# Softmax over rows of 512: issuing each tile's store in the middle of the next tile's exponentials

## The chip, the cores and the metric

The kernel runs on one core of a Trainium2 chip. The metric is the device time in microseconds (us). A profile covers one execution; its span is about 1.7 us shorter than the timed figure of the same run (160.3 against 162.04 us in the profiled run of the kernel before), because it counts from the first to the last profiled event.

## The reference

```python
x = randn(16, 1024, 512)                     # float32
s = x / 0.5
e = exp(s - max(s, axis=-1))
out = e / sum(e, axis=-1)                    # float32
```

16,384 rows of 512 numbers are read and written once: 33.55 MB in, 33.55 MB out.

## The kernel before

The rows are eight chunks (c) of 128 partitions x 16 rows, 4 MB each. Six buffers hold them, so chunks 6 and 7 reuse the buffers of chunks 0 and 1, and their loads wait until stores 0 and 1 have landed. VectorE takes each row's maximum (`shift`), ScalarE the exponentials with their sums, one row at a time, VectorE the reciprocals and the scaling of 7/8 of the rows, ScalarE the scaling of the rest. Loads are issued from the sync engine's queue (q1 in the profile), stores from ScalarE's (q10), as an instruction in ScalarE's own program. So the place of the store in that program decides when it can go out at the earliest.

```python
LOADS = [[(0, 4), (4, G)]] + [WHOLE] * 7
BLOCKS = [[(0, 4), (4, 8), (8, G)]] + [WHOLE] * 6 + [[(0, 8), (8, G)]]
STORES = [WHOLE] * 8
...
def rows(i):
    c, lo, hi = blocks[i]
    cut = hi - lo - (2 if c == 1 else 0)
    return range(cut), range(cut, hi - lo)

exponentials(0, rows(0)[0])
for i in range(n):
    if i + 1 < n:
        exponentials(i + 1, rows(i + 1)[0])   # ScalarE, rows ahead of the cut
    scale_vector(i)                           # VectorE: reciprocal, multiply
    scale_scalar(i)                           # ScalarE: the last 1/8 of the rows
    if i + 2 < n:
        shift(i + 2)                          # VectorE: maximum, bias
    store(i)                                  # issued from ScalarE
    if i + 1 < n:
        exponentials(i + 1, rows(i + 1)[1])   # ScalarE, rows behind the cut
```

## Time and profile before

| | kernel before |
|---|---|
| time, median of its first 3 runs | 162.27 us (162.05 to 162.5) |
| span of the profile | 160.3 us |
| VectorE busy, ScalarE busy | 134.6 us, 102.2 us |
| both DMA queues, share of the span | 49.4% + 48.5% |
| moved | 67.13 MB, 419 GB/s over the span |

A row of 40 digits gives the busy share of each fortieth of the span in tenths (9 is 90% or more). The chain that ended last is the work followed back from the last instruction, at each step to what released it; the line gives its time by engine. In an instruction line the columns are start, duration, engine (DVE is VectorE, ACT ScalarE, SPq and ACTq the queues of issued DMAs), source line, operation, output <- input, shapes, count; a bracket at the end tells how long the engine had been idle and what ended the wait. A queue's line gives packets, MB and the share of the 16 DMA engines' time; a packet counts where it starts, so the share of a short window can be a tenth or two off, and over 100%. A DMA issue's line ends with its size and the microseconds from issue to landing, so landing time is the issue's start plus that figure.

### The profile page before, as it was taken

How to read it: one execution, taken by the hardware profiler on the slowest of the kernel's cores; microseconds unless marked ns; L12 is line 12 of the kernel's file. 1: busy time of each engine (PE TensorE's matmuls, PEld its weight loads, DVE VectorE, ACT ScalarE, POOL GpSimd, SP SyncE). 2: the span in 40 equal slices, each digit the busy share in tenths (PEclk: the TensorE clock that was granted, in tenths of full speed). 3: DMA queues.
4: the chain of work that ended last, by engine and by line, in shares of the span. 5: the costliest groups of instructions: out<-in, count | busy, mean ns of one | idle time of the engine just before them, and what ended most of it. 6: DMA issues, size and time to landing. Idle time of an engine off the chain costs nothing.

```text
span 160.3 us, 402 instructions
## 1 busy us (share of the span) xinstructions
DVE 134.6 (84%) x45; ACT 102.2 (64%) x273; POOL 0.2 (0%) x4
## 2 busy tenths in 40 slices
DVE  0607999999999999999999999999999999957000
ACT  3071549069989972998199909991899891690000
POOL 0000000000000000000000000000000000000000
DMA  5999999999999999999999999999999999999993
GB/s 180 474 409 491 409 401 483 425 393 452 458 393 401 393 425 474 409 393 499 417 393 474 442 393 468 442 393 442 474 393 417 491 401 401 491 417 401 466 442 139
DMA packets 2450, 67.13 MB, mean 419 GB/s; under 512 B 272, under 2 KB 272, under 8 KB 272
## 3 DMA queue, kind: packets, MB, share of 16 engines
q1 hardware_dynamic: 1296, 33.56, 49.4%
q10 hardware_dynamic: 1152, 33.55, 48.5%
q14 instruction: 2, 0.02, 0.0%
HBM read 33.55 MB, written 33.55 MB: 419 GB/s over the span
## 4 chain that ended last, share of the span: by engine, by line
DVE 80%; DMA 7%; ACT 4%; issue 0%; SPq 0%
DVE negmax L74 42%; DVE xt L103 36%; DMA xt<-in_x_dram 7%; ACT xt L86 4%; DVE bias L78 1%; DVE recip L101 1%; SPq L66 0%
## 5 line engine op out<-in xcount | busy, mean ns | idle before, releaser
L86 ACT ACTIVATE xt<-xt,bias 128x512 f32<-128x512 f32 x128 | 90.4, 708 | 41.5 <-DVE bias L78 40.6
L74 DVE TENSOR_REDUCE negmax<-xt 128x16 f32<-128x8192 f32 (+2 forms) x11 | 69.9, 6353 | 9.5 <-DMA xt<-in_x_dram 9.5
L103 DVE TENSOR_TENSOR xt<-xt,recip 128x7168 f32<-128x7168 f32 (+2 forms) x11 | 62.0, 5637 | 0.4
L86 ACT ACTIVATION_READ_ACCUMULATOR xt<-xt,bias 128x1 f32 x128 | 23.9, 187 | 0.0
L112 ACT ACTIVATE xt<-xt,recip 128x512 f32<-128x512 f32 x15 | 9.9, 707 | 0.0
L101 DVE RECIPROCAL recip<-sums 128x16 f32<-128x16 f32 (+2 forms) x11 | 2.4, 218 | 1.8 <-ACT xt L86 1.8
L78 DVE TENSOR_SCALAR bias<-negmax 128x16 f32<-128x16 f32 (+2 forms) x11 | 1.9, 173 | 0.4
L52 ACT ACT_TABLE_LOAD x1 | 1.3, 1283 | 0.7 <-PEq L157 0.7
L51 DVE MEMSET warm<- 128x1 f32 x1 | 0.1, 59 | 0.8 <-PEq L157 0.8
L52 ACT ACTIVATE warm<-warm 128x1 f32<-128x1 f32 x1 | 0.2, 202 | 0.0
L157 POOL MEMSET const-bfloat16-1.0<- 128x1 bf16 x1 | 0.1, 101 | 0.0
L157 POOL MEMSET const-uint8-127<- 128x1 uint8 x1 | 0.1, 101 | 0.0
L157 POOL MEMSET const-float32-0.0<- 128x1 f32 x1 | 0.1, 98 | 0.2 <-issue 0.2
L157 POOL MEMSET const-float32-1.0<- 128x1 f32 x1 | 0.1, 98 | 0.0
## 6 DMA issues: line engine op xcount, KB each, us to landing
out_dram<-xt ACTq DMA_DIRECT2D x8, 4096.0 KB, 22.8
xt<-in_x_dram SPq DMA_DIRECT2D x7, 4096.0 KB, 30.1
xt<-in_x_dram SPq DMA_DIRECT2D x1, 3072.0 KB, 11.7
xt<-in_x_dram SPq DMA_DIRECT2D x1, 1024.0 KB, 4.8
```

Source lines behind the costliest of these rows:

```text
L51: nc.vector.memset(warm, 0.0)
L52: nc.scalar.activation(out=warm, in_=warm, func=EXP)
L74: nc.vector.tensor_reduce(negmax[:, 0:b], chunks[c][:, lo:hi, :], axis=AX, op=MAX, negate=True)
L78: nc.vector.tensor_scalar_mul(biases[i][:, 0:b], negmax[:, 0:b], 2.0)
L86: nc.scalar.activation(out=row, in_=row, func=EXP, bias=biases[i][:, g : g + 1], scale=2.0, accum_out=sums[i][:, g : g + 1],)
L101: nc.vector.reciprocal(recips[i][:, 0:b], sums[i][:, 0:b])
L103: nc.vector.tensor_mul(rows, rows, recips[i][:, 0:k].unsqueeze(2).broadcast_to((P, k, D)))
L112: nc.scalar.activation(out=row, in_=row, func=COPY, scale=recips[i][:, g : g + 1])
L157: nc = _bacc.Bacc("TRN2", target_bir_lowering=False, num_devices=1)
```

## The change

The intent: the store of a chunk (the title's tile) becomes ready once VectorE has scaled its share. The kernel before issues it behind all 16 exponentials of the next chunk (14 for chunk 1). The change cuts the list after 9 rows (5 for chunk 1), about when VectorE is through.

```diff
     def rows(i):
         c, lo, hi = blocks[i]
-        cut = hi - lo - (2 if c == 1 else 0)
-        return range(cut), range(cut, hi - lo)
+        cut = 5 if c == 1 else 9
+        return range(min(cut, hi - lo)), range(min(cut, hi - lo), hi - lo)
```

## The prediction

> **What bounds the kernel now.** I read the page's busy line, then the chain of work that ended last, then the transfers.
>
> ```profile
> DVE 134.6 (84%) x45; ACT 102.2 (64%) x273; POOL 0.2 (0%) x4
> ...
> DVE  0607999999999999999999999999999999957000
> ...
> DMA  5999999999999999999999999999999999999993
> ...
> DVE 80%; DMA 7%; ACT 4%; issue 0%; SPq 0%
> ```
>
> Two resources are full at once. The chain that ended last runs through VectorE (DVE): after 12.8 us it has only one wait of note, 1.8 us for the last exponentials, until the last multiply ends at 147.42 us. The DMA row is nines from the second slice of 4 us to the last but one. The second row is the harder bound: 67.13 MB at 419 GB/s is 160.2 us, the whole span. The chain alone suggests that an earlier store could not matter; the DMA row says that it can't create bandwidth, but can change who gets it.
>
> Next I read the sharing while loads (q1) and stores (q10) are both pending, 50 to 110 us:
>
> ```profile
> DMA packets 894, 26.12 MB, mean 435 GB/s; under 512 B 96, under 2 KB 96, under 8 KB 96
> ...
> q1 hardware_dynamic: 447, 13.07, 50.5%
> q10 hardware_dynamic: 446, 13.04, 50.3%
> ```
>
> The split is equal. So each load of 4 MB takes about 20 us here, where alone it takes about 10. Landing is issue plus time to landing, asked of the transfers in small windows. For the last load, of chunk 7, a window around 87.5 us gives
>
> ```profile
> xt<-in_x_dram SPq DMA_DIRECT2D x1, 4096.0 KB, 28.4
> ```
>
> which is 87.53 + 28.4 = 115.9 us. VectorE first needs that chunk here:
>
> ```profile
> 112.96 7.63 DVE L103 TENSOR_TENSOR xt<-xt,recip 128x7168 f32<-128x7168 f32 x1
> 120.50 4.41 DVE L74 TENSOR_REDUCE negmax<-xt 128x8 f32<-128x4096 f32 x1
> 124.95 0.17 DVE L78 TENSOR_SCALAR bias<-negmax 128x8 f32<-128x8 f32 x1
> 125.03 0.25 DVE L101 RECIPROCAL recip<-sums 128x16 f32<-128x16 f32 x1
> 125.31 7.63 DVE L103 TENSOR_TENSOR xt<-xt,recip 128x7168 f32<-128x7168 f32 x1
> ```
>
> The multiply in front of the reduction is what holds it until 120.50, so the load has 120.50 - 115.9 = 4.6 us to spare. By the same sums load 6 (issued 68.16, 27.7 us) lands at 95.9 and is needed at 103.88: 8.0 us to spare. Loads 1 to 3 land before any store, and loads 4 and 5 at about 57 and 77, needed at 70.65 and 87.26.
>
> At the other end the last two stores are issued at 133.03 and 147.50 and take 16.7 and 11.9 us, so they land at 149.7 and 159.4. The gap, 9.7 us, is a 4 MB transfer at full rate (4.19 MB at 434 GB/s). So at 147.50 the slowest DMA engine still had some 2 us of the store before to finish: the last store found no idle DMA, and VectorE and DMA end almost level.
>
> **What the Trainium skill says.** "DMA: Bandwidth & Descriptors", section "Queues, rings and completion order", says that each DMA engine serves the queues that have work in turn, packet by packet; the 50.5% against 50.3% agrees. Its section "Anatomy of one DMA" says that a DMA's semaphore wait is taken on the issuing sequencer before dispatch. So a store placed among ScalarE's (ACT's) exponentials holds up those behind it until VectorE's multiply is done. The trace of before has such a wait once: the last store's, 3.9 us behind the multiply that starts at 143.53; there nothing follows it. "ScalarE: Activation LUTs", section "What ACT_TABLE_LOAD costs", gives 280 ns + 0.833 ns per element for an ACTIVATE with a pointer bias, 706 ns at 512; the trace has 708.
>
> **The change, part by part.** No instruction is added or removed. Only the place at which ScalarE's list of exponentials of the next block is cut changes: 9 of 16 rows before the two copies and the store, 7 after. For chunk 1 it is 5 of 16 in place of 14. Blocks of 4 or 8 rows stay whole, so the stores of chunks 6 and 7 keep their place in the program.
>
> - Store 0: a row advances ScalarE by 0.705 us (708 + 187 ns, less the overlap; 16 rows from 46.33 to 57.62). Nine rows fewer lie before it, 9 x 0.705 = 6.35 us. It is issued at 44.11 - 6.35 = 37.76, and the multiply that it waits for ends at 37.49: no wait.
> - Stores 1 to 5: seven rows fewer, 4.9 us. Store 1: nine rows from 46.33 end at 52.7, two copies end at 54.0, the multiply ends at 54.10, so issue at about 54.2 in place of 58.97. The remaining seven rows then end at about 59.6, still before the next bias at 62.74. ScalarE waited 4.0 us for that bias before, so its lost time there is hidden.
> - Chunk 6 is the exception. Its successor is a half block, whose reduction takes 4.41 us instead of 8.68. Nine rows from 112.81 end at 119.2, copies at 120.5, the store waits for the multiply (end 120.59), issue 120.67 to 121.05, seven rows more (4.94 us) end at about 126.05. VectorE's reciprocal stands at 125.03 and needs these sums. So it waits some **1.0 us**, where before the sums were there at 124.1.
> - Loads: from the time at which store 0 begins, they get half the rate. It begins 6.35 us earlier and the store queue stays full (stores are issued every 16.6 us and take 19.4 at half rate). In 6.35 us loads lose half of what they moved, and later win it back at half rate: the end of the load stream moves by 6.35 us, one for one. Load 7: 115.9 + 6.35 = 122.25, against 120.50: a wait of **1.75 us**. Load 6: 102.25 against 103.88, still in time by 1.6. The buffers are no limit: store 0 lands at about 62 and store 1 at 81, so loads 6 and 7 can be issued before their forerunners are through.
>
> The two delays don't add. A reduction that starts at 122.25 ends at 126.66, and the reciprocal that follows finds its sums ready at 126.05. So VectorE's chain is late by the larger one, 1.75 us, and the last store is issued at about 149.25 instead of 147.50. The bytes moved up to then are the same in any order, so store 6 still lands near 149.7 to 150. The last store then arrives at a nearly idle DMA. If it lost nothing it would land at 150 + 9.7 = 159.7; if it starts cold, it takes what the first chunk took from nothing, 12.8 - 0.73 = 12.07 us, and lands at 161.3. So the end moves by 0.3 to 1.9 us. I take 1.5, as the issue at 149.25 leaves under 1 us of cover for a start-up of about 2.4 (12.07 - 9.7): 162.27 + 1.5 = **163.8 us**.
>
> **The rivals.**
> 1. *Earlier stores fill idle DMA time and the kernel gets faster.* For it speaks the idle share of the two queues, 100 - 49.4 - 48.5 = 2.1%, 3.4 us. Against it: most of that is the start, before 1.1 us plus latency, and the tail after 158 us, where only completions are left. Between 13 and 147 us hardly a window has a DMA share under 0.95. It would give at most some 0.5 us, so 161.8.
> 2. *The load of chunk 7 stays in time, and only ScalarE's late sums count.* If stores take hold less strongly, so that the load moves under 5 us, then VectorE loses 1.0 us and the end moves by 0 to 1.0: about 162.8. The load's margin, 4.6 against a shift of 6.35, makes this the less likely case.
> 3. *Loads 6 and 7 both come late, or the longer mixed phase costs bandwidth.* The mixed phase grows by about 13 us (6.35 at each end). Its 435 GB/s is that of stores alone (4.19 MB in 9.7 us, 434), so little speaks for that. With 1.6 us of margin gone on load 6 and 2 us more on load 7 it would be 165 to 166.
> 4. *ScalarE becomes the bound because it stalls at each store.* It is busy 64%, and has about 4 us to spare in each full block against a stall of 0.2: excluded except at chunk 6.
>
> **Range and chances.** Rival 1 gives 161.8, rival 2 162.8, the main path 162.6 to 164.2, rival 3 165 or more; the runs of before spread 0.45 us. Range 162.1 to 165.0. Faster by 2% means under 159.0, less than the transfers alone need: 0.01. Slower by 2% means over 165.5, which takes rival 3: 0.05. Within 2%: 0.94.
>
> **What the changed profile would show.** Store 0 issued near 37.8, stores 1 to 5 each about 4.9 us earlier than now. Load 7 landing near 122.2. In VectorE's waits a new one on the input transfer at chunk 7's first reduction, about 1.75 us; if that is absent, a wait of the reciprocal on ScalarE of about 1.0 us near 126. The last store issued near 149.2 with landing after 12 us. DMA still nines, 417 GB/s or so. The prediction is wrong if the mixed phase has another rate than the pure ones, if the equal split does not begin with the issue of store 0, or if the last store's start-up is hidden after all.

## The result, and the profile after

| | before | after |
|---|---|---|
| median time | 162.33 us (6 runs) | 163.36 us (6 runs, 163.13 to 163.59) |
| ratio | | 1.0063, 95% interval 1.005 to 1.0076 |
| span of the profile | 160.3 us | 161.4 us |
| store 0 issued | 44.11 us | 37.69 us |
| load 7 landed | 115.9 us | 122.4 us |
| last store issued, landed | 147.50, 159.4 us | 149.48, 160.6 us |

A ratio here is the mean time of one kernel's fast runs over that of the other's of the same rounds, so it is not quite the ratio of the medians. The changed kernel is slower by about 1.0 us: within 2%, but clear of the noise. The issues of store 0 and of the last store, in the kernel before and in the changed one:

```profile
44.11 0.38 ACTq L120 DMA_DIRECT2D out_dram<-xt  x1
...
147.50 0.34 ACTq L120 DMA_DIRECT2D out_dram<-xt  x1
```

```profile
37.69 0.37 ACTq L120 DMA_DIRECT2D out_dram<-xt  x1
...
149.48 0.34 ACTq L120 DMA_DIRECT2D out_dram<-xt  x1
```

From the page (the summary of the profile) of the changed kernel, the busy line, the rows of 40 slices and the chain that ended last:

```profile
DVE 134.7 (83%) x45; ACT 102.8 (64%) x273; POOL 0.2 (0%) x4
...
DVE  0608999999999999999999999999986999959000
...
DMA  5999999999799999999999999999999999997996
...
DMA 49%; DVE 38%; ACT 4%; issue 0%; SPq 0%; ACTq 0%
```

Busy times are those of before: no work came or went. What changed is the chain. It was 80% VectorE; now DMA has 49% of it. In order of time it runs from VectorE's multiply of chunk 1 over store 1 to the load of chunk 7, which had to wait for that store's buffer, and back to VectorE:

```profile
46.40 7.64 DVE xt L103
...
54.12 27.89 DMA out_dram<-xt
...
82.12 40.33 DMA xt<-in_x_dram
...
122.48 4.43 DVE negmax L74
```

This must not be read as if a faster store 1 would cure it. The load of chunk 7 was issued 5.4 us earlier than before (82.12 against 87.53), and still landed 6.5 us later; it spent the time queued behind load 6 and sharing with stores. VectorE's row has its only new dip, an 8 and a 6, in the two slices from 117.0 to 125.1 us. VectorE's instructions there:

```profile
112.89 7.63 DVE L103 TENSOR_TENSOR xt<-xt,recip 128x7168 f32<-128x7168 f32 x1
122.48 4.42 DVE L74 TENSOR_REDUCE negmax<-xt 128x8 f32<-128x4096 f32 x1 [1.97 <-DMA xt<-in_x_dram]
126.94 0.17 DVE L78 TENSOR_SCALAR bias<-negmax 128x8 f32<-128x8 f32 x1
127.02 0.24 DVE L101 RECIPROCAL recip<-sums 128x16 f32<-128x16 f32 x1
```

The reduction of chunk 7 began at 120.50 in the kernel before without a wait; now it waits 1.97 us for its input. The reciprocal behind it follows at once.

The transfers answer to the lines that the prediction read of before. From small windows around 82.1 and 149.5 us, the last load and the last store of the changed kernel:

```profile
xt<-in_x_dram SPq DMA_DIRECT2D x1, 4096.0 KB, 40.3
```

```profile
out_dram<-xt ACTq DMA_DIRECT2D x1, 4096.0 KB, 11.1
```

So load 7 landed at 82.12 + 40.3 = 122.4 us and the last store at 149.48 + 11.1 = 160.6. Sharing itself is nearly as before (50.5% and 50.3% from 50 to 110 us); in the window from 46 to 110 us the queues of the changed kernel moved

```profile
q10 hardware_dynamic: 470, 13.83, 50.3%
q1 hardware_dynamic: 469, 13.80, 50.0%
```

### The profile page after: what moved, and what is told of

It reads as the page before. It is cut to its first block, busy times and chain, and to the rows that moved or that the text cites. A ratio compares the mean times of both kernels' runs of the same rounds, so it can differ in the third digit from the quotient of the medians.

```text
span 161.4 us, 402 instructions
## 1 busy us (share of the span) xinstructions
DVE 134.7 (83%) x45; ACT 102.8 (64%) x273; POOL 0.2 (0%) x4
## 4 chain that ended last, share of the span: by engine, by line
DMA 49%; DVE 38%; ACT 4%; issue 0%; SPq 0%; ACTq 0%
DMA xt<-in_x_dram 32%; DVE negmax L74 20%; DMA out_dram<-xt 17%; DVE xt L103 17%; ACT xt L86 4%; DVE bias L78 1%; DVE recip L101 1%; SPq L66 0%; ACTq L120 0%
```

## The experiments

Theory, as it stood before these runs: both DMA queues together are the bound, and they share equally. From the moment that the first store begins, loads run at half rate, and the store queue never runs empty afterwards. So the place of **store 0 alone** sets the time at which load 7 lands, one for one; VectorE then waits for it, and the last store is late. Rivals: the other early stores (1 to 5) take the bandwidth; the rows put behind store 5 delay the sums of chunk 6; or the time is lost in the transfers themselves. Each kernel was correct and ran beside the kernel before on the same chip.

### Store 0 back, stores 1 to 5 early

```diff
-        cut = 5 if c == 1 else 9
+        cut = 14 if c == 1 else 9
```

> The changed kernel with chunk 1 cut at 14 rows again, so that store 0 alone goes back to 44.1 us; stores 1 to 5 stay 4.9 us early. Theory (the start of the first store moves the end of the load stream one for one): load 7 lands at 116 us, no wait for it at 120.5; in its place the reciprocal waits 1.0 us for ScalarE near 126, the last store is issued near 148.5 and lands some 11.1 us later: 162.5 us, 0.2 over the kernel before. Rival (the earlier stores 1 to 5 take the bandwidth): load 7 still lands after 119 us, DVE still waits for it, about 163.3 us.

Measured: 162.37 us against 162.31, ratio 1.0003 (0.9991 to 1.0015). Store 0 went out at 44.15, load 7 landed at 116.2, VectorE did not wait for it, and the delay by ScalarE that the prediction had worked out appeared where the load's wait no longer hid it:

```profile
120.53 4.41 DVE L74 TENSOR_REDUCE negmax<-xt 128x8 f32<-128x4096 f32 x1
124.98 0.17 DVE L78 TENSOR_SCALAR bias<-negmax 128x8 f32<-128x8 f32 x1
126.17 0.25 DVE L101 RECIPROCAL recip<-sums 128x16 f32<-128x16 f32 x1 [1.01 <-ACT xt L86]
```

So moving store 0 back takes the whole loss away, within the noise; five early stores and a wait of 1.0 us on VectorE cost nothing that can be measured. By which path store 0 does it this run does not tell. The last store, issued 1.1 us late at 148.63, landed 11.1 us later at 159.7, almost where it landed before.

### Store 0 early, stores 1 to 5 back

```diff
-        cut = 5 if c == 1 else 9
+        cut = 5 if c == 1 else 16
```

> The changed kernel with only chunk 1 cut, at 5 rows; stores 1 to 5 go back behind all exponentials. Theory: the store queue is never empty once store 0 has begun, so load 7 still lands at 122.4 us, VectorE waits 1.9 us for it, the time is that of the changed kernel, 163.3 us. Rival (stores 1 to 5 take the bandwidth, or the late sums of chunk 6 cost the time): load 7 lands near 116 to 118, no wait, 162.3 us.

Measured: 162.60 us, ratio 1.003 (1.0009 to 1.0051), between the two answers. Its profiled run was its slowest, 163.72 us, with load 7 landing at 123.0. The same kernel was run again:

> The kernel with only chunk 1 cut, once more: its profiled run was 163.72 us with a wait of 2.6 us for load 7, its five other runs 162.4 to 162.9. If the wait for load 7 varies from run to run here, this profile shows a shorter one in a faster run (under 1.5 us at 162.6). If the wait is always 2 us or more, then a late VectorE costs less in this kernel than in the changed one, and the last store's landing must show why.

Measured: 162.71 us, ratio 1.0027 (1.0014 to 1.004). The profiled run took 162.51 us with a shorter wait. The reduction of chunk 7, from the first and from the second profile:

```profile
122.98 4.42 DVE L74 TENSOR_REDUCE negmax<-xt 128x8 f32<-128x4096 f32 x1 [2.61 <-DMA xt<-in_x_dram]
```

```profile
121.27 4.42 DVE L74 TENSOR_REDUCE negmax<-xt 128x8 f32<-128x4096 f32 x1 [0.81 <-DMA xt<-in_x_dram]
```

So store 0 alone makes load 7 late, as the theory says, but the size of the delay varies between runs of one program, and time goes with it. On average this kernel loses about half of what the changed kernel loses. With stores 1 to 5 back, store 1 is issued only 4.1 to 4.4 us before store 0 lands (8.2 us in the changed kernel), and the theory's "never runs empty" fails here: from 60 to 64 us loads moved 0.95 and 1.02 MB in the two profiles and stores 0.69 and 0.62, where the changed kernel has 0.69 of loads and 1.05 of stores. That this is why the kernel loses less was not isolated; in the first profile load 7 was late all the same. The rival that stores 1 to 5 have a part is thus not excluded for the other half.

### The changed kernel once more

> The changed kernel once more, unaltered. Two other kernels with the same program up to chunk 7 showed waits for load 7 between 0.8 and 2.6 us, so this tells how far one profile of it can be trusted. If the wait of 2.0 us belongs to the change: again 1.8 to 2.2 us and 163.3 us. If the wait varies from run to run: another wait, and a time that goes with it (0.8 us with about 162.6).

Measured: 163.36 us, ratio 1.0056 (1.0037 to 1.0075). The profile shows a wait of 2.27 us, a little above the 1.8 to 2.2 expected, in a run of 163.35 us. So a wait of about 2 us was seen in both profiles of the changed kernel. One of its six runs took 162.47 us; that one has no profile, so whether it waited less is not known.

### Store 0 at two other times

Two kernels fill in the line: store 0 half way, with chunk 6 left whole so that its sums are never late, and no cut at all.

```diff
-        cut = 5 if c == 1 else 9
+        cut = 10 if c == 1 else 16 if c == 6 else 9
```

> The changed kernel with chunk 1 cut at 10 rows, chunk 6 whole. Theory of one for one: store 0 is issued near 41.3, 2.8 us before its place in the kernel before, load 7 lands near 118.9, within its margin of 120.5, so VectorE waits for nothing, the reciprocal follows at 125.0, 162.4 us. Rival (the shift is not one for one but a fixed loss when the stores come early): load 7 near 116 or near 122.

```diff
-        cut = 5 if c == 1 else 9
+        cut = 16
```

> The changed kernel with no cut at all: every store behind all exponentials, store 0 near 45.4 us. Theory of one for one: load 7 lands near 114.6, VectorE waits for nothing, and since the transfers set the end and the last store is covered, 162.3 us. If each us of shared reading and writing costs transfer time, this has the shortest such stretch and is some 0.1 us faster than before, within noise.

Measured: 162.39 us, ratio 1.0016 (0.9996 to 1.0036), with one slow run of 163.3; and 162.17 us, ratio 0.9992 (0.998 to 1.0004). Neither has a wait for load 7.

| kernel | store 0 issued | load 7 landed | shift against before |
|---|---|---|---|
| no cut | 45.63 us | 114.0 us | store 1.5 later, load 1.9 earlier |
| before | 44.11 | 115.9 | |
| store 0 half way | 41.16 | 118.5 | store 3.0 earlier, load 2.6 later |
| changed | 37.69 | 122.4 | store 6.4 earlier, load 6.5 later |

Over the range the load moves by about what the store moves, but not exactly: in the five profiles with store 0 near 37.6 us and load 7 whole, the store stands 6.4 to 6.6 us earlier than before and the load lands 5.3 to 7.1 us later. The wait appears only where load 7 passes 120.5 us.

### Load 7 in halves, so that its first reduction need not wait

```diff
-    LOADS = [[(0, 4), (4, G)]] + [WHOLE] * 7
+    LOADS = [[(0, 4), (4, G)]] + [WHOLE] * 6 + [[(0, 8), (8, G)]]
```

> The changed kernel with the load of chunk 7 in two halves, so that the first reduction needs only 2 MB. Theory: first half lands near 113 us, second near 122.4; no wait at 120.5; the late sums of chunk 6 come to the surface as a wait of the reciprocal of 1.0 us near 126; last store near 148.5; 162.5 us. Rival (the time is lost in the transfers themselves, not in VectorE's wait): still 163.3 us.

With that, and chunk 6 not cut (`16 if c == 6`):

> As the run with the load of chunk 7 in halves, and chunk 6 not cut (all 16 rows ahead of store 5). Theory: neither wait is left, the reciprocal follows at 125.0, last store at 147.5 as in the kernel before, 162.3 us: all of the loss is undone although stores 0 to 4 are early; and nothing is gained over before, since the transfers fill the span. Rival (early stores gain once the waits are mended): clearly under 162.0 us.

Measured: 162.77 us, ratio 1.0038 (1.0025 to 1.0051), and 162.55 us, ratio 1.0019 (1.0007 to 1.0031). The waits moved as expected: in the first the wait for load 7 is gone and the reciprocal waits 1.01 us for ScalarE; in the second neither is left, and the last store went out at 147.29. The landings did not: 113 and 122.4 us were expected in the first, 117.1 and 131.6 were seen. And both kernels are clearly over before, which the second was not expected to be. The halves themselves were measured in the kernel before, with the same edit and nothing else:

> The kernel before with the load of chunk 7 in halves and nothing else. It measures what the halves cost in themselves, since the run with early stores and no VectorE wait left was 0.24 us over the kernel before. If the halves cost it: 162.5 us here. If the longer stretch in which loads and stores share costs it: 162.3 us here, as before.

Measured: 162.97 us, ratio 1.0037 (1.0022 to 1.0051), with VectorE's waits as before and the last store at 147.51. So the halved load costs some 0.4% by itself, as much as or more than the two kernels above lose. They show where the waits come from, but their times can't be set against the changed kernel's to price a wait.

The late landings (111.4 and 126.2 us in this last kernel, where the whole load lands at 115.9) show what "equal sharing" means. From 104 to 116 us, with stores whole and the load in halves:

```profile
q10 hardware_dynamic: 109, 3.57, 68.9%
q1 hardware_dynamic: 112, 1.57, 30.6%
```

The queues take turns by packets, not by bytes: about as many packets of each, but the packets of a halved load hold 16 KB and those of a whole one 32 KB, so the load gets under a third of the bytes. Why this costs 0.6 us at the end was not found.

### The last store in halves

```diff
-    STORES = [WHOLE] * 8
+    STORES = [WHOLE] * 7 + [[(0, 8), (8, G)]]
```

In the changed kernel:

> The changed kernel with the last store in two halves, the first issued when VectorE and ScalarE have scaled rows 0 to 7 of chunk 7. Theory (the late last store finds the DMA engines nearly idle and pays part of a start-up): VectorE still waits 2.0 us for load 7, the second half is issued near 149.5 as before, but the first half goes out near 145.9 and keeps the queue full, so the last byte lands near 159.9 instead of 160.6: 162.7 us. Rival (VectorE's delay passes whole to the end, whatever the DMA does): 163.3 us.

In the kernel before:

> The kernel before with only the last store in halves. Theory (before, the last store is covered by the one ahead of it, so no start-up is left to hide): no gain, 162.3 us, last byte near 159.4. If the halves themselves cost transfer time: 162.5 to 162.6 us, which would then account for what the changed kernel with the last store in halves has left over before. Rival (a start-up is exposed in the kernel before too): under 161.9 us.

Measured: 162.55 us, ratio 1.0022 (1.001 to 1.0033), and 162.41 us, ratio 1.0003 (0.9991 to 1.0015). Here the DMA share tells why the first loses less than the changed kernel (ratio 1.0022 against 1.0063). The windows from 147 to 151 us (length, busy time of VectorE, ScalarE and GpSimd with instruction counts, clock, DMA share, GB/s), first of the changed kernel, then of the changed kernel with the last store in halves:

```profile
147.00:151.00 4.00, 2.41 (x1) 0.00 (x0) 0.00 (x0) 1.00 0.63 270
```

```profile
147.00:151.00 4.00, 1.63 (x1) 0.00 (x0) 0.00 (x0) 1.00 0.97 418
```

In the changed kernel the DMA engines were short of work there: 37% of 4 us, 1.5 us on average, or 1.3 us if packets are cut at the window's ends. With halves the first 2 MB went out at 145.11 (and landed 9.9 us later, the second, issued at 148.71, after 11.2 us, at 159.9) and the queue stayed full, although VectorE still waited for load 7 (1.27 us in this run, less than in the changed kernel, so part of the gain in the profiled run is the shorter wait). The kernel before has nothing to gain from it, as its last store was covered already.

Some 0.2% remains over before with the last store in halves. The packet records tell where it lies, though no run isolates it. The times of all packets, summed and divided by 16 engines, give 157.1 us in the kernel before and 157.6 in this one for the same bytes; their last packets end at 159.06 and 159.57. The longer packets are those of loads, just ahead of store 0's first packet: 1.40 us per 32 KB from 36 to 44 us in the changed kernel (1.22 before, which has its own slow stretch of 1.46 from 44 to 48), against 1.21 almost everywhere else. The sum is 157.1 to 157.3 in the five profiles with store 0 at 44 us or later, 157.3 with it half way, and 157.5 to 157.9 in the seven with it near 37.6. So the rival that time is lost in the transfers themselves has a part in every kernel with an early store 0, by these sums 0.5 to 0.8 us of transfer time; why the slow stretch costs more when it comes earlier was not tested.

None of the kernels tried is shown to be faster than the kernel before. The one with no cut has the lowest median, and its interval includes 1.

## Why the prediction was right

The prediction was right in sign, in its main mechanism (store 0, load 7, VectorE's wait, the late last store) and within its range: 163.36 us against 163.8 (162.1 to 165.0).

- **The bound.** Right: with packets cut at the windows' ends, their time fills all 16 DMA engines of the changed kernel in every stretch from 13 to 146 us, and no kernel with early stores beat the one before. (Read by the view, "hardly a window has a DMA share under 0.95" is not so: 11 of the 33 windows of 4 us from 13 to 145 us show 0.87 to 0.94, and others up to 1.16, as packets count where they start.)
- **The equal split begins with the issue of store 0.** Not so, and the prediction had named this as a sign of being wrong: store 0's first packet came 4.2 us after its issue before (48.28) and 4.5 us in the changed kernel (42.22). The time of load 7 came out all the same, as the delay was nearly the same in both. Loads ran slower in that stretch, which the prediction did not foresee.
- **Store 0 at 37.76.** Measured 37.69; stores 1 to 5 at 54.12 and every 16.6 us after, as worked out.
- **Load 7 at 122.25, VectorE waiting 1.75 us.** Measured 122.4 and 1.97 us. Four times of store 0 agree with one for one. That the figure is so close is in part luck: waits of 0.8 to 2.6 us were seen with store 0 at this place.
- **Two delays that don't add.** Right: the late sums of chunk 6 are hidden in the changed kernel and show as 1.01 us, against a worked-out 1.0, where load 7 comes in time.
- **The last store at 149.25.** Measured 149.48.
- **The end 1.5 us later.** Too much; about 1.0 us was measured. The term that was mis-sized is the start-up of the last store: "a start-up of about 2.4 (12.07 - 9.7)", taken from the first chunk's load at the very start, which is in two parts and so no like case. The store landed 11.1 us after its issue, 1.4 over 9.7, and did so in the changed kernel, in its repeat and in the kernel with store 0 back. With 11.1 for 12.07 the prediction's own sum gives 149.25 + 11.1 - 159.4, about 0.95 us, or 163.2.
- **Rivals.** Idle DMA time to be filled, the first, was not there. Rival 2's wait of 1.0 us was real, but cost nothing by itself. Load 6 was in time (103.1 for 103.8), so rival 3's second wait did not come. Its other half, that the mixed phase costs bandwidth, did not come either in the phase itself (1.22 us per 32 KB from 60 to 110 us in the changed kernel, 1.21 before, 1.21 for stores alone); only the slow stretch at its start costs some.

The same 11.1 us explains which delays are free. In the kernel before the last store lands at 159.4, 11.9 us after its issue, because it queues behind the store before it. It could be issued up to about 0.8 us later at no cost; the wait of 1.0 us on ScalarE's sums fits nearly into that, the 2 us on load 7 do not.

## What to carry to other kernels

Where the transfers fill the span, issuing one earlier can't add bandwidth; it takes it from the others, so ask which of those has the least time to spare, and compare that with the shift. Equal sharing, which holds for packets of one size, makes this a simple sum: the end of the load stream moved by about as much as the start of the store stream (6.5 us for 6.4 in the first profile), until it passed the moment at which its consumer was ready. And a last transfer that starts on idle DMA engines pays its start-up, 1.4 us here: issuing half of it earlier kept the engines full in this kernel.

## What the Trainium skill lacked or had wrong

- "DMA: Bandwidth & Descriptors" puts the fixed cost of a DMA at about 2.0 us, with a fit for GpSimd-issued ones. For a 4 MB store issued from ScalarE as the DMA ran out of work, 11.1 us against 9.7 at full rate were seen, 1.4 us; the first chunk's load, from nothing and in two parts, had 2.4. Beyond a first-byte latency the page has no figure for a start on a queue that is about to run dry.
- The same page gives round-robin sharing, which this trace confirms (50.5% and 50.3%), but not what follows for a schedule: the load stream ends later by as much as the store stream starts earlier (6.5 us for 6.4 in the first profile, 5.3 to 7.1 in all). Nor does it say that taking turns by packets gives a load of half-size packets about a third of the bytes, as seen here: 1.57 MB against 3.57.
- The same page's rule for the most bandwidth is 128 partitions and 1 MiB or more per DMA. Splitting one 4 MB load of eight into two of 2 MB, late in the shared stretch, cost 0.37% of the time (0.6 us); splitting the last store the same way cost 0.03%, within noise. Both halves are above 1 MiB. The smaller share of the halved load is shown above, but not that it causes the loss.
- No page says that one program's load may land at times 1.8 us apart in two runs: 123.0 and 121.2 us in two profiles of the kernel with store 0 alone early.
